# Three small matrix-product jobs inside an attention block are re-cut: compression in two runs, compressed scores with the keys held in the array, high and low values side by side

## The chip, the core and the metric

The kernel runs on one core of a Trainium2 chip. The core has a matrix engine (TensorE: PE in the profile, with PEld for its weight loads), a vector engine (DVE), a scalar engine (ACT), GpSimd (POOL) and a queue engine that issues transfers (SP). The metric is device microseconds of the whole program, one launch. Before the change the median of three runs is 1295.36 us (1295.05 to 1295.36).

A matrix product holds one operand in the 128x128 array (the stationary one, brought in by a weight load) and streams the other past it; the sum goes to one of eight banks of PSUM.

## The reference

Two layers of a transformer trunk on 256 tokens of width 1024, all in fp32. Each layer does, in this order: a gated feed-forward block, an attention block with three branches, a second feed-forward block and a small gated input. The time of this case is decided in the attention block:

```python
ya = diff_attention(aq, ak, av, ...)   # A: 4 heads, two softmaxes each, values 128 wide, then a norm per head
yb = nsa_attention(...)                # B: 8 heads in 2 groups: compressed + selected + window attention
yc = swa_sink_attention(cq, ck, cv)    # C: 8 heads in 2 groups, window 128, sinks
merged = sigmoid(ga)*(ya@w0) + sigmoid(gb)*(yb@w1) + sigmoid(gc)*(yc@w2)
h = h + merged @ w_out
```

The compressed part of B takes blocks of 32 tokens (step 16, so 15 blocks) of its keys and of its values, adds a position, multiplies each by a 2048x256 matrix, applies gelu and multiplies by a 256x64 matrix:

```python
k_cmp = gelu((blocks(kc) + pos[0]) @ cmp_w1[0]) @ cmp_w2[0]      # and the same for the values
p_c = masked_softmax(q . k_cmp * scale + bias, dist_c >= 0)
o_c = p_c @ v_cmp
```

## The kernel before

**Precision.** Most products are made of three: each operand is split into a high and a low part (type fp32r), and `mul3` (lines 264 to 267) adds high x high, high x low and low x high. ACT makes the high part by a copy (line 258), DVE the low part by a subtraction (line 253). A few products, the compression among them, are done on plain fp32 operands instead; the trace shows each of those as two matrix instructions.

**Main line and side lines.** The large products of the attention block (projections A0, A1, A2, Ck, Cq, Bk, Bv, Bq, then for each branch the gate and the branch product, two column halves each, then the output product) are emitted one after the other by `product`. After each step of three matrix instructions it calls `flow.tick()`. `Flow` (line 186) holds side lines, which are Python generators: at each tick a lane gets `pace` more credit, and for every whole credit one step (up to the next `yield`) of its first side line is emitted. Lane 0 holds the attention of A, then C, then B, with paces `PACE_A`, `PACE_C`, `PACE_B` (line 47); lane 1 holds the compressed part with pace 1. `flow.join` emits what is left of a side line when its result is needed.

The order in which things are emitted is their priority. A planner then sets the order on each engine: it goes through a simulated time line and takes, on each engine, the instruction of best priority whose operands and buffers are free. `tc.high_priority(offset=n)` moves an instruction n places ahead in priority, and `keep_in_program_order` keeps it behind the one before it. On the chip each engine then works through its own list in order.

**Weights.** All streamed weights go through one list, `queue`, fetched in its order (`fetch`, line 303), at least `AHEAD` places in front of their use. A streamed piece (512 KB) lands in one of 4 `raw` tiles by a transfer on SP, and its high and low part go to one `wh` and one `wl` tile, 6 of each (`WBUFS`). The eight pieces of the compression matrix (`Whole`, line 382) are not split: they land directly in `wh` tiles (even pieces) and `wl` tiles (odd pieces). They enter the list behind other pieces: `Weights.push` (lines 288 to 292) takes one of them for every second piece of Bv, Bq and what follows.

**Compression** (`compressing`, line 1181). The tile `e` (token blocks with the position added) is stationary in quarters of the array: 32 columns at a time, so that key and value and two successive row blocks go to the four column groups. For each of the eight weight pieces, as soon as it is there, four fp32 products of 256 columns are emitted (line 1202), then the side line yields. All add up in one PSUM bank (`cmp`), one of three with the tag `tp`. Then follow gelu and the second matrix (`compressed`, line 1207), and the compressed keys `kbd` are split into high and low, `kt`.

**Compressed scores** (`attend_cmp`, line 1280), once per half of the tokens (`t` = 0, 1): four `mul3` with the queries stationary (128x128) and 32 columns of keys streaming, then bias, softmax and gate on DVE and ACT at [128, 8, 16], a transpose by the matrix engine (`pct`) and a copy to `pcT[t]`, which the attention of B waits for.

**Values of A** (`attend_a`, `second`, line 1093). For each of four units (head pair m, token half t), and for each of two heads and t + 1 key blocks, one `mul3` with the transposed probabilities stationary and 128 value columns streaming, into the single bank with the tag `y`. Then two squares with row sums straight from that bank (line 1107), mean and power -1/2 (POOL, line 1109), the scaling out of the bank (line 1110), two transposes (`yt`) and a split.

**Scores of A, B and C** (`scores`, line 996) use the array in two row halves of 64 and write twelve products to two banks (tag `s`). The first has its natural priority, the other eleven are 300 places ahead and kept in order.

Of the kernel before, what the change touches and what calls it, by code (L numbers as in the profile page):

```python
# [43 lines left out]
LATE_ON = False  # L44
FLIPS = ["flip"]
POINTS = (5, 8, 11, 14, 18, 21)
PACE_A, PACE_B, PACE_C = 0.8, 0.8, 0.8

# [166 lines left out]
def trunk(ctx: ExitStack, tc: tile.TileContext, a: dict, out: bass.AP, index: list):  # L217
# [24 lines left out]
    def y_bank(name):  # L242
        return bank("y", 1, name)
# [20 lines left out]
    def mul3(ps, xh, xl, wh, wl, start, stop, **kw):  # L264
        nc.tensor.matmul(ps, xh, wh, start=start, stop=False, **kw)  # L265
        nc.tensor.matmul(ps, xh, wl, start=False, stop=False, **kw)  # L266
        nc.tensor.matmul(ps, xl, wh, start=False, stop=stop, **kw)  # L267
# [10 lines left out]
    class Weights:  # L278
# [9 lines left out]
        def push(self, j):  # L288
            self.at[j] = len(queue)
            queue.append(lambda: self.tiles.__setitem__(j, load(*self.pieces[j], 2 if self.at[j] < 2 else 1, j in self.apart)))  # L290
            if extra and j % 2 == 0:
                extra.pop(0)()

        def __call__(self, k):
# [659 lines left out]
    def attention(i, norm, after):  # L954
# [116 lines left out]
        def attend_a():  # L1071
            bnd = band(0)

            def first(u):
                m, t = u
                nk = 128 * (t + 1)
                s = scores("s", qk[m], [0, 1], t, lambda x, r, k: qk[m][r, x, 2 + k, :nk])
                yield
                p = pool.tile([128, 4, 256], F32, tag="p", bufs=3, name="p")
                st = None  # L1080
                for st in softmax([p[:, j, :nk] for j in range(4)], [s[j // 2][:, j % 2, :nk] for j in range(4)],
                                  [back(bnd[:, 2 * m + j % 2], nk) for j in range(4)]):
                    yield
                nc.vector.reciprocal(st[:, 8:12], st[:, 4:8])
                nc.vector.tensor_scalar(st[:, 10:12], st[:, 10:12], nlam[:, i:i + 1], None, op0=ALU.mult)
                for x in range(2):
                    nc.vector.tensor_scalar(p[:, 2 + x, :nk], p[:, 2 + x, :nk], st[:, 10 + x:11 + x], None, op0=ALU.mult)
                    nc.vector.scalar_tensor_tensor(p[:, x, :nk], p[:, x, :nk], st[:, 8 + x:9 + x], p[:, 2 + x, :nk],
                                                   op0=ALU.mult, op1=ALU.add)
                yield  # L1090
                return p

            def second(u, p):
                m, t = u
                T = turned([p[:, x, k * 128:(k + 1) * 128] for k in range(t + 1) for x in range(2)])
                yield
                y_ps = y_bank("ya")[:, :256]
                for x in range(2):
                    o, hd = slice(x * 128, x * 128 + 128), slice((2 * m + x) * 128, (2 * m + x + 1) * 128)
                    for k in range(t + 1):  # L1100
                        mul3(y_ps[:, o], T[:, 0, 2 * k + x, :], T[:, 1, 2 * k + x, :], va[0][:, 0, k, hd], va[0][:, 1, k, hd], k == 0, k == t)
                    yield
                y = pool.tile([128, 256], F32, tag="yt", bufs=2, name="yn")
                st = pool.tile([128, 32], F32, tag="st", bufs=4, name="st")
                for x in range(2):
                    o = slice(x * 128, x * 128 + 128)
                    nc.scalar.activation(y[:, o], y_ps[:, o], AF.Square, accum_out=st[:, x:x + 1])
                nc.vector.tensor_scalar(st[:, 2:4], st[:, 0:2], 1.0 / 128, EPS, op0=ALU.mult, op1=ALU.add)
                nc.gpsimd.tensor_tensor(st[:, 4:6], st[:, 2:4], mhalf[:, :2], op=ALU.pow)
                nc.vector.tensor_tensor(y.rearrange("p (h e) -> p h e", h=2), y_ps.rearrange("p (h e) -> p h e", h=2),  # L1110
                                        st[:, 4:6, None].to_broadcast([128, 2, 128]), op=ALU.mult)
                yield
                if m == 0:
                    yA[t] = y_tile("yA")
                ps = tp_bank("yt")
                transposes(ps, [y[:, x * 128:x * 128 + 128] for x in range(2)])
                split(yA[t][:, 0, 2 * m:2 * m + 2], yA[t][:, 1, 2 * m:2 * m + 2],
                      ps[:, :256].rearrange("p (k q) -> p k q", k=2), sg[:, i:i + 1])
                yield

            yield from pipelined([(m, t) for m in range(2) for t in range(NT)], first, second)


# [57 lines left out]
        def compressing():  # L1181
            pos = pool.tile([128, 2, 2, 8], F32, name="pos")
            nc.sync.dma_start(pos, a["pos"][i].rearrange("p (v s j) -> p v s j", v=2, s=2))
            e = base.tile([128, 2, 2, 8, 32], F32, tag="blk", bufs=6, name="e")
            yield
            nc.vector.memset(e[:, :, 1, :, 31:32], 0.0)
            for kv in range(2):
                for s in range(2):
                    nc.vector.tensor_tensor(
                        e[:, kv, s, :, 0:32 - s],  # L1190
                        half[0][:, 2 * kv:2 * kv + 2, :].rearrange("p g (n j) -> p j (g n)", j=8)[:, :, s:],
                        pos[:, kv, s, :, None].to_broadcast([128, 8, 32 - s]), op=ALU.add)
                yield
            c_ps = bank("tp", 3, "cmp")
            for j in range(8):
                while not w1.ready(j, 3):
                    yield
                w = w1(j)
                for x in range(4):
                    k, kv = 2 * j + x // 2, x % 2  # L1200
                    q = 32 * (2 * (k % 2) + kv)
                    nc.tensor.matmul(c_ps[q:q + 32, :256], e[:, kv, k // 8, k % 8], w[:, 256 * x:256 * x + 256], start=j == 0, stop=j == 7)
                yield
            c_sb[0] = pool.tile([128, 256], F32, name="c_sb")
            nc.vector.tensor_copy(c_sb[0], c_ps[:, :256])

        def compressed():
# [29 lines left out]
            kv_ = k_ps[:, :32].rearrange("p (g n) -> p g n", g=2)  # L1237
            nc.vector.tensor_copy(kbd[0:64, :, 0:16], kv_[0:64])
            nc.vector.tensor_copy(kbd[64:128, :, 16:32], kv_[64:128])
            kt = pool.tile([128, 2, 2, 32], F32R, name="kc")  # L1240
            split(kt[:, 0], kt[:, 1], kbd)
            yield
            v_ps = tp_bank("vc")
            rows_ = base.tile([128, 2, 2, 128], F32R, tag="stage", bufs=4, name="rows")
# [9 lines left out]
            yield  # L1254
            vc[0] = pool.tile([128, 1, 128], F32R, name="vc")
            values(vc[0], v_ps[:, :64], None)
            kc[0] = kt
            yield
            for t in range(NT):
                yield from attend_cmp(t)  # L1260

        def weighted(y_ps, v, T, start, stop):

# [13 lines left out]

        yB, pcT, readyB = [None] * NT, {}, [0] * NT

        def attend_cmp(t):  # L1280
            s_ps = tp_bank("sc")
            for j in range(4):
                mul3(s_ps[:, 32 * j:32 * j + 32], qB[0][:, 0, j, t * 128:(t + 1) * 128], qB[0][:, 1, j, t * 128:(t + 1) * 128],
                     kc[0][:, 0, j // 2], kc[0][:, 1, j // 2], True, True)
            yield
            p = pool.tile([128, 8, 16], F32, tag="pc", bufs=2, name="pc")
            st = pool.tile([128, 32], F32, tag="st", bufs=4, name="st")
            nc.vector.tensor_tensor(p, s_ps[:, :128].rearrange("p (h n) -> p h n", h=8), cbias[:, t], op=ALU.add)
            nc.vector.tensor_reduce(st[:, 0:8], p, axis=AX.X, op=ALU.max)
            nc.vector.tensor_tensor(p, p, st[:, 0:8, None].to_broadcast([128, 8, 16]), op=ALU.subtract)  # L1290
            nc.scalar.activation(p, p, AF.Exp)
            yield
            nc.vector.tensor_reduce(st[:, 8:16], p, axis=AX.X, op=ALU.add)
            nc.vector.reciprocal(st[:, 8:16], st[:, 8:16])
            nc.vector.tensor_tensor(st[:, 0:8].rearrange("p (g a b) -> p g a b", g=2, a=2),
                                    st[:, 8:16].rearrange("p (g a b) -> p g a b", g=2, a=2),
                                    sig[t][:, 0:8].rearrange("p (g b a) -> p g a b", g=2, a=2), op=ALU.mult)
            nc.vector.tensor_tensor(p, p, st[:, 0:8, None].to_broadcast([128, 8, 16]), op=ALU.mult)
            nc.vector.tensor_tensor(p, p, cmask[:, None, t, :].to_broadcast([128, 8, 16]), op=ALU.mult)
            yield  # L1300
            ps = tp_bank("pct")
            transposes(ps, [p.rearrange("p h n -> p (h n)")])
            pcT[t] = pool.tile([128, 128], F32, tag="pcT", bufs=2, name="pcT")
            nc.scalar.activation(pcT[t], ps[:, :128], AF.Copy)
            yield

        def own(t, g):
# [453 lines left out]
```

## Time and profile before

| what | value |
|---|---|
| median of 3 runs | 1295.36 us |
| the profiled execution, its own time | 1295.46 us |
| its span (first to last instruction) | 1293.7 us |
| matrix instructions in it | 6250 |
| TensorE clock granted, mean | 0.998 |
| stretch with the side lines, layer 1, about | 210 to 420 us of the span |
| stretch with the side lines, layer 2, about | 847 to 1057 us of the span |

In the views, an instruction group is named by line, engine, operation, output and inputs. In the timeline the first number is the start and the second the time that the group is in flight. Matrix instructions are pipelined, so a new one starts long before the last one ends; what one costs the engine is the distance from its start to the start of the next.

### The profile page before, as it was taken

How to read it: one execution, taken by the hardware profiler on the slowest of the kernel's cores; microseconds unless marked ns; L12 is line 12 of the kernel's file. 1: busy time of each engine (PE TensorE's matmuls, PEld its weight loads, DVE VectorE, ACT ScalarE, POOL GpSimd, SP SyncE). 2: the span in 40 equal slices, each digit the busy share in tenths (PEclk: the TensorE clock that was granted, in tenths of full speed). 3: DMA queues.
4: the chain of work that ended last, by engine and by line, in shares of the span. 5: the costliest groups of instructions: out<-in, count | busy, mean ns of one | idle time of the engine just before them, and what ended most of it. 6: DMA issues, size and time to landing. Idle time of an engine off the chain costs nothing.

```text
span 1293.7 us, 17861 instructions
## 1 busy us (share of the span) xinstructions
PE 1283.7 (99%) x6250; PEld 1052.7 (81%) x6250; DVE 1069.8 (83%) x1736; ACT 907.8 (70%) x1450; POOL 27.5 (2%) x46
## 2 busy tenths in 40 slices
PE   9999999999999999999999999999999999999997
PEld 7888888877878888888888888888778788888886
DVE  7878977666788799997799999777677978999975
ACT  6778667577587487876667876676765866787664
POOL 0000000000000000000000000000000000000000
PEclk9999999999999999999999999999999999999999
DMA  8778788465534568687666787865654435678772
GB/s 320 230 232 269 206 243 224 165 237 167 189 118 129 175 185 244 212 241 214 212 195 237 201 250 229 250 180 200 224 178 144 140 130 194 206 202 240 237 222 83
DMA packets 137179, 263.73 MB, mean 204 GB/s; under 512 B 71670, under 2 KB 77174, under 8 KB 137088
## 3 DMA queue, kind: packets, MB, share of 16 engines
q1 hardware_dynamic: 134128, 252.56, 63.4%
q0 software_dynamic: 2528, 9.47, 2.2%
q8 instruction: 49, 0.80, 0.3%
q10 hardware_dynamic: 432, 0.56, 0.1%
q14 instruction: 42, 0.34, 0.1%
HBM read 245.74 MB, written 1.08 MB: 191 GB/s over the span
## 4 chain that ended last, share of the span: by engine, by line
PE 99%; issue 0%; DVE 0%; ACT 0%; POOLq 0%; POOL 0%; DVEq 0%; ACTq 0%
PE ff L266 8%; PE ff L265 8%; PE ff L267 8%; PE fo L267 5%; PE fo L265 5%; PE fo L266 5%; PE p L265 4%; PE p L267 4%; PE p L266 4%; PE gate L265 4%; PE gate L266 4%; PE gate L267 4%; PE s L1008 2%; PE br L265 2%; PE A L266 2%; PE A L267 2%
## 5 line engine op out<-in xcount | busy, mean ns | idle before, releaser
L253 DVE TENSOR_TENSOR wl<-raw,wh 128x1024 fp32r<-128x1024 f32 (+1 forms) x410 | 491.8, 1213 | 85.2 <-ACT wh L258 84.2
L258 ACT ACTIVATE wh<-raw 128x1024 fp32r<-128x1024 f32 (+1 forms) x410 | 424.7, 1048 | 155.0 <-DMA raw<-in_wst 59.1
L266 PE MATMUL ff<-wl,nT 128*128 128x512 f32 x464 | 180.9, 390 | 0.0
L267 PE MATMUL ff<-wh,nT 128*128 128x512 f32 x464 | 180.3, 390 | 0.0
L265 PE MATMUL ff<-wh,nT 128*128 128x512 f32 x464 | 171.7, 390 | 0.0
L267 PE MATMUL fo<-wh,gT 128*128 128x512 f32 x304 | 117.1, 390 | 0.0
L266 PE MATMUL fo<-wl,gT 128*128 128x512 f32 x304 | 115.7, 389 | 0.0
L265 PE MATMUL fo<-wh,gT 128*128 128x512 f32 x304 | 114.3, 390 | 0.0
L266 PEld LDWEIGHTS ff<-wl,nT 128*128 128x128 f32 x464 | 87.1, 188 | 18.2 <-DVE wl L253 0.3
L265 PEld LDWEIGHTS ff<-wh,nT 128*128 128x128 f32 x464 | 87.1, 188 | 18.0
L267 PEld LDWEIGHTS ff<-wh,nT 128*128 128x128 f32 x464 | 87.1, 188 | 17.9
L265 PE MATMUL gate<-wh,nT 128*128 128x512 f32 x192 | 78.3, 408 | 0.0
L266 PE MATMUL gate<-wl,nT 128*128 128x512 f32 x192 | 76.8, 400 | 0.0
L267 PE MATMUL gate<-wh,nT 128*128 128x512 f32 x192 | 76.8, 402 | 0.0
L267 PEld LDWEIGHTS fo<-wh,gT 128*128 128x128 f32 x304 | 57.1, 188 | 11.8
L266 PEld LDWEIGHTS fo<-wl,gT 128*128 128x128 f32 x304 | 57.1, 188 | 11.8
L265 PEld LDWEIGHTS fo<-wh,gT 128*128 128x128 f32 x304 | 57.1, 188 | 11.7
L1021 ACT ACTIVATE p<-p,st 128x128 f32<-128x128 f32 (+1 forms) x128 | 56.6, 446 | 13.2 <-DVE st L1019 12.1
L606 ACT ACTIVATE whole<-flip 128x1024 uint16<-128x1024 uint16 x32 | 43.0, 1367 | 20.9 <-DMA flip<-cut 20.9
L600 ACT ACTIVATE cut<-gated 128x1024 uint16<-128x1024 uint16 (+1 forms) x48 | 46.3, 974 | 8.6 <-DVE gated L646 8.6
L253 DVE TENSOR_TENSOR wl<-x,wh 128x1024 fp32r<-128x1024 f32 x42 | 50.5, 1224 | 2.0 <-ACT wh L258 2.0
L258 ACT ACTIVATE wh<-x 128x1024 fp32r<-128x1024 f32 x42 | 43.8, 1049 | 5.7 <-DVE x L253 4.5
(391 smaller groups left out, 2734.0 us busy)
## 6 DMA issues: line engine op xcount, KB each, us to landing
raw<-in_wst SPq DMA_DIRECT2D x408, 512.0 KB, 4.4
w<-in_wst SPq DMA_DIRECT2D x16, 512.0 KB, 4.6
y<-in_wst POOLq DMA_DIRECT2D x6, 1024.0 KB, 6.6
band<-table SPq DMA_DIRECT2D x10, 512.0 KB, 4.7
xy<-in_wst POOLq DMA_DIRECT2D x4, 512.0 KB, 4.1
raw<-in_wbv SPq DMA_DIRECT2D x4, 420.0 KB, 3.1
xt<-in_xt SPq DMA_DIRECT2D x4, 256.0 KB, 5.5
raw<-in_wst SPq DMA_DIRECT2D x4, 256.0 KB, 5.2
```

The costliest lines, as they stand in the source:

```text
L253: nc.vector.tensor_tensor(o, x, y, op=ALU.subtract)
L258: nc.scalar.activation(hi, src, AF.Copy)
L265: nc.tensor.matmul(ps, xh, wh, start=start, stop=False, **kw)
L266: nc.tensor.matmul(ps, xh, wl, start=False, stop=False, **kw)
L267: nc.tensor.matmul(ps, xl, wh, start=False, stop=stop, **kw)
L600: nc.scalar.activation(cut.rearrange("p (w n) -> p w n", w=2), halves(src)[:, :128 * m].rearrange("p n w -> p w n"), AF.Copy)
L606: tc.keep_in_program_order(nc.vector.tensor_copy(to, of) if late else nc.scalar.activation(to, of, AF.Copy))
L1008: ins = nc.tensor.matmul(o, q[r, x, qb[m], t * 128:(t + 1) * 128], kk, start=x + y == 0, stop=x == 1)
L1021: nc.scalar.activation(p[j], p[j], AF.Exp, bias=st[:, j:j + 1], scale=-1.0, accum_out=st[:, n + j:n + j + 1])
```

## The change

Five edits, all but the first two inside the attention block's side lines:

1. The paces become 0.75 (A), 0.9 (B) and 1.178 (C) instead of 0.8 each.
2. `Weights.push` takes a piece of the compression matrix with every piece pushed, instead of every second one. The list is then Bv0 w0 Bv1 w1 Bv2 w2 Bq0 w3 Bq1 w4 Bq2 w5 Bq3 w6 and, behind the first gate piece, w7; before, the last pieces stood among those of the second gate.
3. The compression waits for four pieces and then emits sixteen products at once, twice; all but the first of each sixteen are 600 places ahead in priority and kept in program order.
4. The compressed scores are made once for both token halves: keys `kbd` (fp32, 32 columns) are stationary in the four column groups, and the high and then the low queries of all 256 tokens stream past, read as plain fp32. The scores come out with heads and blocks on partitions; ACT copies them out, the matrix engine transposes them back (two transposes, new), and bias, softmax, gate, mask, transposes and copy run once at [128, 2, 8, 16].
5. The values of A: the high probabilities are stationary for high and low values side by side (256 columns, two results), then the low ones for the high values (128 columns). ACT copies the low result out, DVE adds the high one; squares and scaling then read the sum from SBUF instead of PSUM.

```diff
-PACE_A, PACE_B, PACE_C = 0.8, 0.8, 0.8
+PACE_A, PACE_B, PACE_C = 0.75, 0.9, 1.178
...
-            if extra and j % 2 == 0:
+            if extra and j % 1 == 0:
...
-                        mul3(y_ps[:, o], T[:, 0, 2 * k + x, :], T[:, 1, 2 * k + x, :], va[0][:, 0, k, hd], va[0][:, 1, k, hd], k == 0, k == t)
+                        nc.tensor.matmul(y_ps[:, x], T[:, 0, 2 * k + x, :], va[0][:, :, k, hd], start=k == 0, stop=False, skip_group_check=True)
+                        nc.tensor.matmul(y_ps[:, x, 0], T[:, 1, 2 * k + x, :], va[0][:, 0, k, hd], start=False, stop=k == t, skip_group_check=True)
...
+                nc.scalar.activation(yv, y_ps[:, :, 1], AF.Copy)
+                nc.vector.tensor_tensor(yv, yv, y_ps[:, :, 0], op=ALU.add)
...
-            for j in range(8):
-                while not w1.ready(j, 3):
+            for b in range(0, 8, 4):
+                while not w1.ready(b + 4 - 1, 3):
                     yield
...
+                        with tc.high_priority(offset=600 if (k, kv) != (2 * b, 0) else 0):
+                            ins = nc.tensor.matmul(c_ps[q:q + 32, :256], e[:, kv, k // 8, k % 8], w[k // 2 - b][:, o:o + 256], start=k < 2, stop=k >= 14)
+                        if (k, kv) != (2 * b, 0):
+                            tc.keep_in_program_order(ins)
...
-        def attend_cmp(t):
+        def attend_cmp():
             s_ps = tp_bank("sc")
-            for j in range(4):
-                mul3(s_ps[:, 32 * j:32 * j + 32], qB[0][:, 0, j, t * 128:(t + 1) * 128], qB[0][:, 1, j, t * 128:(t + 1) * 128],
-                     kc[0][:, 0, j // 2], kc[0][:, 1, j // 2], True, True)
+            for x in range(2):
+                for j in range(4):
+                    with tc.high_priority(offset=0 if x == j == 0 else 300):
+                        ins = nc.tensor.matmul(s_ps[32 * j:32 * j + 32, :SEQ], kc[0][:, j // 2], qB[0][:, x, j].bitcast(F32), start=x == 0, stop=x == 1)
+                    if (x, j) != (0, 0):
+                        tc.keep_in_program_order(ins)
...
+            nc.scalar.activation(sc, s_ps[:, :SEQ], AF.Copy)
+            yield
+            ps = tp_bank("st")
+            transposes(ps, [sc[:, t * 128:(t + 1) * 128] for t in range(NT)])
```

More of the change, by code (lines that the diff above doesn't have):

```diff
@@ L1096, in second @@
                 yield
-                y_ps = y_bank("ya")[:, :256]
+                y_ps = y_bank("ya").rearrange("p (h x e) -> p h x e", h=2, x=2)
                 for x in range(2):
-                    o, hd = slice(x * 128, x * 128 + 128), slice((2 * m + x) * 128, (2 * m + x + 1) * 128)
+                    hd = slice((2 * m + x) * 128, (2 * m + x + 1) * 128)
                     for k in range(t + 1):
-                        mul3(y_ps[:, o], T[:, 0, 2 * k + x, :], T[:, 1, 2 * k + x, :], va[0][:, 0, k, hd], va[0][:, 1, k, hd], k == 0, k == t)
+                        nc.tensor.matmul(y_ps[:, x], T[:, 0, 2 * k + x, :], va[0][:, :, k, hd], start=k == 0, stop=False, skip_group_check=True)
+                        nc.tensor.matmul(y_ps[:, x, 0], T[:, 1, 2 * k + x, :], va[0][:, 0, k, hd], start=False, stop=k == t, skip_group_check=True)
                     yield
@@ L1104, in second @@
                 st = pool.tile([128, 32], F32, tag="st", bufs=4, name="st")
+                yv = y.rearrange("p (h e) -> p h e", h=2)
+                nc.scalar.activation(yv, y_ps[:, :, 1], AF.Copy)
+                nc.vector.tensor_tensor(yv, yv, y_ps[:, :, 0], op=ALU.add)
+                sq = pool.tile([128, 256], F32, tag="ysq", bufs=1, name="sq")
                 for x in range(2):
                     o = slice(x * 128, x * 128 + 128)
-                    nc.scalar.activation(y[:, o], y_ps[:, o], AF.Square, accum_out=st[:, x:x + 1])
+                    nc.scalar.activation(sq[:, o], y[:, o], AF.Square, accum_out=st[:, x:x + 1])
                 nc.vector.tensor_scalar(st[:, 2:4], st[:, 0:2], 1.0 / 128, EPS, op0=ALU.mult, op1=ALU.add)
                 nc.gpsimd.tensor_tensor(st[:, 4:6], st[:, 2:4], mhalf[:, :2], op=ALU.pow)
-                nc.vector.tensor_tensor(y.rearrange("p (h e) -> p h e", h=2), y_ps.rearrange("p (h e) -> p h e", h=2),
-                                        st[:, 4:6, None].to_broadcast([128, 2, 128]), op=ALU.mult)
+                nc.vector.tensor_tensor(yv, yv, st[:, 4:6, None].to_broadcast([128, 2, 128]), op=ALU.mult)
                 yield
@@ L1194, in compressing @@
             c_ps = bank("tp", 3, "cmp")
-            for j in range(8):
-                while not w1.ready(j, 3):
+            for b in range(0, 8, 4):
+                while not w1.ready(b + 4 - 1, 3):
                     yield
[L1198 to L1202, printed above, removed]
+                w = [w1(j) for j in range(b, b + 4)]
+                for k in range(2 * b, 2 * b + 2 * 4):
+                    for kv in range(2):
+                        q, o = 32 * (2 * (k % 2) + kv), 256 * (2 * (k % 2) + kv)
+                        with tc.high_priority(offset=600 if (k, kv) != (2 * b, 0) else 0):
+                            ins = nc.tensor.matmul(c_ps[q:q + 32, :256], e[:, kv, k // 8, k % 8], w[k // 2 - b][:, o:o + 256], start=k < 2, stop=k >= 14)
+                        if (k, kv) != (2 * b, 0):
+                            tc.keep_in_program_order(ins)
                 yield
@@ L1239, in compressed @@
             nc.vector.tensor_copy(kbd[64:128, :, 16:32], kv_[64:128])
-            kt = pool.tile([128, 2, 2, 32], F32R, name="kc")
-            split(kt[:, 0], kt[:, 1], kbd)
             yield
@@ L1256, in compressed @@
             values(vc[0], v_ps[:, :64], None)
-            kc[0] = kt
+            kc[0] = kbd
             yield
-            for t in range(NT):
-                yield from attend_cmp(t)
+            yield from attend_cmp()
         def weighted(y_ps, v, T, start, stop):
@@ L1278, in attention @@
         yB, pcT, readyB = [None] * NT, {}, [0] * NT
-        def attend_cmp(t):
+        def attend_cmp():
             s_ps = tp_bank("sc")
-            for j in range(4):
-                mul3(s_ps[:, 32 * j:32 * j + 32], qB[0][:, 0, j, t * 128:(t + 1) * 128], qB[0][:, 1, j, t * 128:(t + 1) * 128],
-                     kc[0][:, 0, j // 2], kc[0][:, 1, j // 2], True, True)
-            yield
-            p = pool.tile([128, 8, 16], F32, tag="pc", bufs=2, name="pc")
-            st = pool.tile([128, 32], F32, tag="st", bufs=4, name="st")
[L1288 to L1291, printed above, removed]
-            yield
[L1293 to L1299, printed above, removed]
@@ new lines, in attend_cmp @@
+            for x in range(2):
[4 more added lines that the diff above has]
+                        tc.keep_in_program_order(ins)
+            yield
+            sc = pool.tile([128, SEQ], F32, tag="sc", bufs=1, name="sc")
+            nc.scalar.activation(sc, s_ps[:, :SEQ], AF.Copy)
@@ new lines, in attend_cmp @@
+            yield
+            ps = tp_bank("st")
+            transposes(ps, [sc[:, t * 128:(t + 1) * 128] for t in range(NT)])
+            yield
+            p = pool.tile([128, NT, 8, 16], F32, tag="pc", bufs=1, name="pc")
+            st = pool.tile([128, 32], F32, tag="st", bufs=4, name="st")
+            flat = p.rearrange("p t h n -> p (t h) n")
+            nc.vector.tensor_tensor(flat, ps[:, :SEQ].rearrange("p (h n) -> p h n", n=16), cbias.rearrange("p t h n -> p (t h) n"), op=ALU.add)
@@ new lines, in attend_cmp @@
+            nc.vector.tensor_reduce(st[:, 0:16], flat, axis=AX.X, op=ALU.max)
+            nc.vector.tensor_tensor(flat, flat, st[:, 0:16, None].to_broadcast([128, 16, 16]), op=ALU.subtract)
+            nc.scalar.activation(flat, flat, AF.Exp)
+            yield
+            nc.vector.tensor_reduce(st[:, 16:32], flat, axis=AX.X, op=ALU.add)
+            nc.vector.reciprocal(st[:, 16:32], st[:, 16:32])
+            for t in range(NT):
+                nc.vector.tensor_tensor(st[:, 8 * t:8 * t + 8].rearrange("p (g a b) -> p g a b", g=2, a=2),
+                                        st[:, 16 + 8 * t:24 + 8 * t].rearrange("p (g a b) -> p g a b", g=2, a=2),
+                                        sig[t][:, 0:8].rearrange("p (g b a) -> p g a b", g=2, a=2), op=ALU.mult)
@@ L1300, in attend_cmp @@
+            yield
+            nc.vector.tensor_tensor(flat, flat, st[:, 0:16, None].to_broadcast([128, 16, 16]), op=ALU.mult)
+            nc.vector.tensor_tensor(p, p, cmask[:, :, None, :].to_broadcast([128, NT, 8, 16]), op=ALU.mult)
             yield
             ps = tp_bank("pct")
-            transposes(ps, [p.rearrange("p h n -> p (h n)")])
-            pcT[t] = pool.tile([128, 128], F32, tag="pcT", bufs=2, name="pcT")
-            nc.scalar.activation(pcT[t], ps[:, :128], AF.Copy)
+            transposes(ps, [p[:, t].rearrange("p h n -> p (h n)") for t in range(NT)])
@@ L1305, in attend_cmp @@
+            both = pool.tile([128, NT, 128], F32, tag="pcT", bufs=1, name="pcT")
+            nc.scalar.activation(both.rearrange("p t q -> p (t q)"), ps[:, :SEQ], AF.Copy)
+            for t in range(NT):
+                pcT[t] = both[:, t]
             yield
```

## The prediction

> **What bounds the kernel now.** I read the page first, then who waited for whom, then the stretches, and at the end the timeline of TensorE around the lines that the change touches.
>
> ```profile
> span 1293.7 us, 17861 instructions
> PE 1283.7 (99%) x6250; PEld 1052.7 (81%) x6250; DVE 1069.8 (83%) x1736; ACT 907.8 (70%) x1450; POOL 27.5 (2%) x46
> PE 99%; issue 0%; DVE 0%; ACT 0%; POOLq 0%; POOL 0%; DVEq 0%; ACTq 0%
> ```
>
> TensorE is in use through 1283.7 of 1293.7 us, and the chain that ended last is 99% its own: nearly every matrix instruction was released by the one before it. Matrix instructions overlap, so "busy" alone could hide waits. The list of waits, for PE alone, and two stretches rule that out:
>
> ```profile
> PE warm L1703 <- DVE idle L1698: 1.5, 1, 1.5
> ...
> 210.00:420.00 210.00, 210.00 (x1198) 169.57 (x1197) 160.11 (x401) 148.16 (x344) 2.77 (x4) 1.00 0.53 170
> ...
> 847.00:1057.00 210.00, 210.00 (x1198) 169.67 (x1197) 160.35 (x401) 148.13 (x344) 2.77 (x4) 1.00 0.53 170
> ```
>
> The only wait is at the start of the program. The stretches that hold the side lines (columns: length, PE, PEld, DVE, ACT, POOL, clock, DMA share, GB/s) have the same counts in both layers, so what one costs is counted twice. DVE is free for 50 of 210 us there, ACT for 62, the transfers for half. So the time is the sum of the distances from one matrix start to the next, and I cost the change in these distances.
>
> **Compression in two runs.** The timeline of PE:
>
> ```profile
> 282.82 1.91 PE L1202 MATMUL cmp<-w,e 128*32 128x256 f32 x26
> 284.67 0.32 PE L1008 MATMUL s<-kC,qC 64*128 64x128 f32 x1
> 284.92 0.64 PE L1202 MATMUL cmp<-w,e 128*32 128x256 f32 x8
> 285.49 0.88 PE L1008 MATMUL s<-kC,qC 64*128 64x128 f32 x11
> 286.30 0.63 PE L1202 MATMUL cmp<-w,e 128*32 128x256 f32 x6
> 286.86 0.50 PE L265 MATMUL gate<-wh,nT 128*128 128x512 f32 x1
> ...
> 288.42 0.62 PE L1202 MATMUL cmp<-w,e 128*32 128x256 f32 x2
> ...
> 289.39 0.63 PE L1202 MATMUL cmp<-w,e 128*32 128x256 f32 x6
> ...
> 299.51 0.64 PE L1202 MATMUL cmp<-w,e 128*32 128x256 f32 x8
> ...
> 308.06 0.63 PE L1202 MATMUL cmp<-w,e 128*32 128x256 f32 x6
> ...
> 312.38 0.40 PE L267 MATMUL gate<-wh,nT 128*128 128x512 f32 x1
> 312.71 0.62 PE L1202 MATMUL cmp<-w,e 128*32 128x256 f32 x2
> 313.26 0.50 PE L265 MATMUL gate<-wh,nT 128*128 128x512 f32 x1
> 313.59 0.40 PE L266 MATMUL gate<-wl,nT 128*128 128x512 f32 x1
> 313.82 0.39 PE L267 MATMUL gate<-wh,nT 128*128 128x512 f32 x1
> ```
>
> The 64 records of a layer (32 products, two each) fall into eight runs. A run of 2, 6 or 8 records lasts 0.55, 0.56 or 0.57 us to the next start (312.71 to 313.26, 286.30 to 286.86, 284.92 to 285.49): up to four products go through the four column groups side by side, and one costs as much as four. A run of 26 lasts 1.85: three full groups of 8 and a run of 2, so a full group inside a run costs (1.85 - 0.55) / 3 = 0.43. Each run also lengthens its neighbours: the gate before takes 0.33 (312.38 to 312.71) and the one after 0.33 (313.26 to 313.59) where a gate takes 0.23 (313.59 to 313.82). That is 0.10 at each edge.
>
> Before, per layer: the block from 282.82 to 286.86 is 4.04, with outer edges 4.24; in it is one set of scores of C, whose last eleven take 0.81 and which, whole and with edges, I put at 1.02. This leaves 3.22. The other five runs (2, 6, 8, 6, 2) are 2.79 and with edges 3.79. Together 7.01. After: a run of 32 is 3 x 0.43 + 0.57 = 1.86, with edges 2.06, two of them 4.12. Saved 2.89 a layer, **5.8 us** in both. Less, if runs break (a rival below).
>
> **Compressed scores.** Before, 24 instructions a layer, in two blocks of twelve:
>
> ```profile
> 350.06 0.26 PE L265 MATMUL sc<-kc,qB 128*128 128x32 f32 x1
> ...
> 351.40 0.48 PE L265 MATMUL gate<-wh,nT 128*128 128x512 f32 x1
> ```
>
> Twelve take 1.34, so 0.112 each and 2.69 a layer. After, eight fp32 products of the compression's shape (32 columns stationary, 256 streaming): one run of two groups, 0.43 + 0.57 = 1.00, with edges 1.20; and two more transposes. Four transposes are 0.36 (248.19 to 248.55, quoted next), two 0.18. Saved 2.69 - 1.38 = 1.31 a layer, **2.6 us**. I take the compression's row because the shape is the same; the bounds are two groups side by side as there, or all eight one by one at a lone product's 0.55 (4.4 + 0.2, a loss of 2.1 a layer). The row of the same shape decides.
>
> In the Trainium skill ("TensorE: Matmul & The Clock Gate", section "Measured speedup vs the span model") three column tiles give 2.38 times, 0.79 of the ideal. By that a group would cost 0.43 / 0.79 = 0.54, and the 20 groups of the new runs in both layers 20 x 0.11 = 2.2 us more than I count (an estimate). The trace has four products for the price of one, and goes before it.
>
> **High and low values side by side.**
>
> ```profile
> 248.19 0.60 PE L273 MATMUL qt<-ident,stage 128*128 128x128 f32 x4
> 248.55 0.31 PE L265 MATMUL ya<-va,pT 128*128 128x128 f32 x1
> ...
> 249.92 0.45 PE L267 MATMUL Bk<-wh,nT 128*128 128x512 f32 x1
> ```
>
> ```profile
> 222.90 0.28 PE L265 MATMUL Ck<-wh,nT 128*128 128x256 f32 x1
> 223.02 0.28 PE L266 MATMUL Ck<-wl,nT 128*128 128x256 f32 x1
> ```
>
> A `mul3` of 128 columns is 3 x 0.114 = 0.34 (twelve instructions from 248.55 to 249.92). A product of 256 columns costs 0.12 (the Ck row), so the pair costs 0.12 + 0.11 = 0.23. There are 12 a layer (2 pairs x 2 heads x 1 + 2 key blocks): saved 1.3 a layer, **2.6 us**; other ya blocks run a little closer than 0.114, so I take 2.4. That the 256 columns come from two places is not in the trace: the bounds are 0.11 (as for 128) and 0.23 (as for 512), which moves 2.4 between 2.6 and -0.2.
>
> It adds, per unit and eight times in all, a copy on ACT and an add on DVE, at 128x256 out of PSUM:
>
> ```profile
> L1110 DVE TENSOR_TENSOR yn<-ya,st x8: 416/425/458, 237.0 to 916.9; 128x256 f32<-128x256 f32 x8
> ```
>
> About 0.43 each, 3.4 us on each engine, between the last ya instruction and the yt transposes. The main products hide them on PE and the 50 and 62 free us on DVE and ACT; without that cover it is 0.85 a unit, 6.8 us. The softmax of the compressed part becomes one chain of wider operations where two stood, and the split of the keys falls away: fewer instructions on DVE, off the path, nothing. The bank of the values comes free earlier, before POOL's power instead of after it.
>
> **Paces and the list of weights.** These two cost nothing by themselves; they move work. The price at stake is a set of scores broken in two:
>
> ```profile
> 279.60 0.38 PE L1008 MATMUL s<-kC,qC 64*128 64x256 f32 x1
> 279.91 0.49 PE L265 MATMUL gate<-wh,nT 128*128 128x512 f32 x1
> 280.34 0.98 PE L1008 MATMUL s<-kC,qC 64*128 64x256 f32 x11
> 281.24 0.50 PE L266 MATMUL gate<-wl,nT 128*128 128x512 f32 x1
> ...
> 392.75 0.38 PE L1008 MATMUL s<-kB,qB 64*128 64x256 f32 x1
> ```
>
> The first product goes alone (0.31), a gate gets in (0.43 instead of 0.23), eleven follow: 0.51 more than a whole set. Between these two rows six of a layer's fourteen sets are broken so (two of C, four of B), beside the one at 284.67 that the compression broke. None of A is. The breaks come where the second bank is free later than the first. Faster paces could bring sets closer to the softmax that frees the banks, or C's work ahead of the crowd with the compression. Bounds: none broken, -12 x 0.51 = -6.1; all broken, +16 x 0.51 = +8.2. From the rows I see no reason for one sign and take 0.
>
> Three transfers of the compression matrix move ahead, past the pieces of Bq and the first gates in SP's list.
>
> ```profile
> raw<-in_wst SPq DMA_DIRECT2D x408, 512.0 KB, 4.4
> ```
>
> The transfers are at 0.53 of their time there, so the move is free on them; what it does to the tiles is the rival on the slow side.
>
> **The sum.** -5.8 - 2.6 - 2.4 = -10.8. The profiled execution took 1295.46 by its own time (1.8 more than its span), 0.1 above the median 1295.36. Forecast: 1295.4 - 10.8 = **1284.6 us**, its own range 1282 to 1287.
>
> **The rivals.**
>
> *Fewer broken sets.* C is done sooner at 1.178 and the compression no longer cuts in, so half or more of the twelve broken sets could become whole; for it speaks that four of A's four are whole, where the banks are not pressed; against it the higher pace of B, which has most breaks. All: 1284.6 - 6.1 = 1278.5.
>
> *The runs break.* As in `scores`, the first product of each new run has its natural priority, and only the rest is pulled ahead. If each of the six runs loses its first product, each costs a lone 0.55 and edges 0.2 more: 6 x 0.75 = 4.5, 1289.1. So the change would not quite do what its words say. For it: half of the score sets break. Against: these write one bank, the sets two, and the weights must be in before the first is emitted.
>
> *The saved time comes back as waiting.* PE gains 10.8 us, and the stretch then hangs on DVE or ACT: 1295.4. Against: 50 free us.
>
> *The tiles run out: slower.* A piece of the compression matrix sits in a `wh` or `wl` tile from its landing to its run. Before, it went as soon as it was in; now four wait for each other, two of the six tiles of each kind, up to three with the next. Bq needs four pieces at once for its two token halves. If the first run is late (it waits for `e`), a piece of Bq or of the first gate finds no tile, SP's list stands behind it, and PE waits for a landing and a split:
>
> ```profile
> L253 DVE TENSOR_TENSOR wl<-raw,wh 128x1024 fp32r<-128x1024 f32 (+1 forms) x410 | 491.8, 1213 | 85.2 <-ACT wh L258 84.2
> L258 ACT ACTIVATE wh<-raw 128x1024 fp32r<-128x1024 f32 (+1 forms) x410 | 424.7, 1048 | 155.0 <-DMA raw<-in_wst 59.1
> ```
>
> 4.4 + 1.05 + 1.21 = 6.7, less the 12 x 0.23 = 2.8 that PE still has from the piece before: 3.9 for each starved piece. With two a layer it is 1284.6 + 15.6 = 1300.2; from three in all it ends slower than before (3 x 3.9 = 11.7 against 10.8). Against: `raw` tiles take landings ahead, and PE can do the second half's products of pieces that are in.
>
> **How the numbers follow.** My forecast 0.56; fewer broken sets 0.17; runs break 0.13; waiting 0.07; tiles 0.07. A measurement here tells about 0.2%, 2.6 us, from no change. Faster holds the first three, 0.86; same 0.07; slower 0.07. The range leaves the last two out (0.14) and ends near the two others and their unknown prices: 1278 to 1290.5.
>
> **What would show it.** Right: 6214 matrix instructions (24 fewer ya, 16 fewer sc, 4 more transposes); the cmp line in four runs of 32, each 1.86 to the next start; sc in two runs of 16 at 1.0; ya pairs 0.12 and 0.11 apart; still no wait on PE. Wrong, if a run of x2 stands alone ahead of one of x30, if PE waits for `wl` or for a transfer between 262 and 300, or if the count of lone s rows moves far from six a layer.

## The result, and the profile after

The changed kernel takes 1285.41 us (median of four runs, 1285.08 to 1285.68) against 1295.36 before (four runs by now, 1295.05 to 1296.23): 9.95 us less, a ratio of 0.9922 with a 95% interval of 0.9905 to 0.9939. The forecast was 1284.6. The page of the changed kernel, whose profiled execution took 1285.68:

```profile
span 1283.9 us, 17792 instructions
PE 1271.9 (99%) x6214; PEld 1044.5 (81%) x6214; DVE 1069.8 (83%) x1728; ACT 908.7 (71%) x1454; POOL 28.9 (2%) x46
...
PE 92%; DMA 2%; ACT 2%; DVE 2%; issue 1%; SPq 0%; POOLq 0%; POOL 0%; DVEq 0%; ACTq 0%
```

There are 6214 matrix instructions, as counted. What is new is the chain that ended last: 8% of it is no longer PE. That is not 8% of lost time. Wherever PE waits, the chain goes back through the engine that it waited for, and most of its pieces off PE lie between 88 and 146 us, far from the change, behind one wait of 0.4 (`fo`, at 146.05). What was lost is in the list of waits of PE (waiting line, what released it, us in total, times, longest):

```profile
PE warm L1721 <- DVE idle L1716: 1.5, 1, 1.5
PE ya L1102 <- DVE pT L253: 0.7, 1, 0.7
PE gate L266 <- DVE wl L253: 0.6, 2, 0.3
PE fo L265 <- ACT wh L258: 0.4, 1, 0.4
PE ff L712 <- ACT nT L469: 0.3, 1, 0.3
PE Bq L265 <- ACT sig L1162: 0.2, 1, 0.2
```

They come to 3.7 us, 1.5 of them at the start of the program. Before, the first of these was the only one. To see where the time went, take in each layer the stretch from the first instruction of the product Ck to the last of the output product. Timeline of PE, before:

```profile
221.01 0.39 PE L265 MATMUL Ck<-wh,nT 128*128 128x256 f32 x1
...
445.22 0.39 PE L267 MATMUL wo<-wh,mT 128*128 128x512 f32 x1
...
1082.15 0.39 PE L267 MATMUL wo<-wh,mT 128*128 128x512 f32 x1
```

and after:

```profile
221.51 0.39 PE L265 MATMUL Ck<-wh,nT 128*128 128x256 f32 x1
...
441.34 0.39 PE L267 MATMUL wo<-wh,mT 128*128 128x512 f32 x1
...
1072.78 0.39 PE L267 MATMUL wo<-wh,mT 128*128 128x512 f32 x1
```

Layer 1 goes from 224.2 to 219.8, layer 2 (its Ck starts at 858.08 before and 854.21 after) from 224.1 to 218.6: 4.4 and 5.5 less, where the working gave 5.4 each. The rest of the program is as it was to half a microsecond.

The three parts in the timeline of the changed kernel. The compression, in layer 1:

```profile
298.61 0.38 PE L1008 MATMUL s<-kC,qC 64*128 64x256 f32 x1
298.93 0.33 PE L273 MATMUL pt<-ident,p 128*128 128x128 f32 x1
299.18 1.93 PE L1207 MATMUL cmp<-w,e 128*32 128x256 f32 x32
301.05 0.97 PE L1008 MATMUL s<-kC,qC 64*128 64x256 f32 x11
...
302.43 1.93 PE L1207 MATMUL cmp<-w,e 128*32 128x256 f32 x32
304.29 0.66 PE L273 MATMUL pt<-ident,p 128*128 128x128 f32 x4
```

Two whole runs of 32 records, 1.87 and 1.86 to the next start, as worked out. The first stands in the middle of a broken set of C's scores. The compressed scores:

```profile
342.55 1.07 PE L1289 MATMUL sc<-qB,kbd 128*32 128x256 f32 x16
343.55 0.50 PE L266 MATMUL br<-wl,yC 128*128 128x512 f32 x1
```

One run of 16 records, 1.00. The values of A, in a unit that runs through and in the one that does not (both layer 1):

```profile
250.45 0.22 PE L1102 MATMUL ya<-va,pT 128*128 128x128 f32 x1
250.51 0.33 PE L1101 MATMUL ya<-va,pT 128*128 128x256 f32 x1
250.68 0.22 PE L1102 MATMUL ya<-va,pT 128*128 128x128 f32 x1
250.74 0.33 PE L1101 MATMUL ya<-va,pT 128*128 128x256 f32 x1
...
263.39 0.28 PE L1101 MATMUL ya<-va,pT 128*128 128x256 f32 x1
264.38 0.33 PE L1102 MATMUL ya<-va,pT 128*128 128x128 f32 x1 [0.71 <-DVE pT L253]
```

A pair costs 0.17 + 0.06 = 0.23 (250.51 to 250.74), the sum that was forecast. At 263.39 the next instruction starts 0.99 later, because the low probabilities are not there. DVE made the low half of a weight piece and a part of B's values first, and these low probabilities only then:

```profile
262.50 1.23 DVE L253 TENSOR_TENSOR wl<-raw,wh 128x1024 fp32r<-128x1024 f32 x1 [1.03 <-ACT wh L258]
...
263.91 0.41 DVE L253 TENSOR_TENSOR pT<-pt,pT 128x256 fp32r<-128x256 f32 x1
```

Layer 2 has no such wait. A second one, at a gate, is in both layers (287.80 here):

```profile
286.88 0.61 PE L265 MATMUL gate<-wh,nT 128*128 128x512 f32 x2
287.80 0.50 PE L266 MATMUL gate<-wl,nT 128*128 128x512 f32 x1 [0.31 <-DVE wl L253]
```

Two starts and the gap after them take 0.92 where two gates take 0.46. What DVE and ACT did before it:

```profile
283.51 1.06 ACT L258 ACTIVATE wh<-raw 128x1024 fp32r<-128x1024 f32 x1 [1.80 <-PE gate L267]
...
284.28 0.67 DVE L1193 TENSOR_TENSOR e<-half,pos 128x256 f32<-128x256 f32 x1 [1.31 <-issue]
...
284.85 1.76 DVE L1193 TENSOR_TENSOR e<-half,pos 128x248 f32<-128x248 f32 x3
286.53 1.22 DVE L253 TENSOR_TENSOR wl<-raw,wh 128x1024 fp32r<-128x1024 f32 x1
```

The high half of the piece came late, after ACT had waited 1.80 for a product of the gate, and its low half then stood on DVE behind the making of the compression's `e`.

### The profile page after: what moved, and what is told of

The parts are those of the page before. It is cut to its first block, busy times and chain, and to the rows that moved or that the text cites. A ratio compares the mean times of both kernels' runs of the same rounds, so it can differ in the third digit from the quotient of the medians.

```text
span 1283.9 us, 17792 instructions
## 1 busy us (share of the span) xinstructions
PE 1271.9 (99%) x6214; PEld 1044.5 (81%) x6214; DVE 1069.8 (83%) x1728; ACT 908.7 (71%) x1454; POOL 28.9 (2%) x46
## 4 chain that ended last, share of the span: by engine, by line
PE 92%; DMA 2%; ACT 2%; DVE 2%; issue 1%; SPq 0%; POOLq 0%; POOL 0%; DVEq 0%; ACTq 0%
PE ff L267 7%; PE ff L266 7%; PE ff L265 7%; PE fo L265 5%; PE fo L266 5%; PE fo L267 5%; PE p L265 4%; PE p L266 4%; PE p L267 4%; PE gate L267 3%; PE gate L266 3%; PE gate L265 3%; PE s L1008 2%; PE br L266 2%; PE br L265 2%; PE A L266 2%
## 5 line engine op out<-in xcount | busy, mean ns | idle before, releaser
L267 PE MATMUL gate<-wh,nT 128*128 128x512 f32 x192 | 76.0, 398 | 0.0
L265 PE MATMUL gate<-wh,nT 128*128 128x512 f32 x192 | 75.2, 399 | 0.0
```

## The experiments

Four kernels carry a part of the change on the kernel before (edits 2 and 3 go together), four are the changed kernel with one edit, or in one case half of edit 3, taken back, and four move the first product of a set of scores. The changed kernel without edit 4 alone was not run. Each ran beside the kernel before on the same chip; ratios are to that. "Stretch" is the two stretches of above taken together: 448.3 us before, 438.4 after. A layer has fourteen sets of scores; broken sets count as two runs, and all runs of a layer are counted, 21 before and 20 after.

**High and low side by side, alone** (edit 5 on the kernel before)

```diff
-mul3(y_ps[:, o], T[..0..], T[..1..], va[0][:, 0, k, hd], va[0][:, 1, k, hd], ...)
+nc.tensor.matmul(y_ps[:, x], T[:, 0, 2 * k + x, :], va[0][:, :, k, hd], ...)
+nc.tensor.matmul(y_ps[:, x, 0], T[:, 1, 2 * k + x, :], va[0][:, 0, k, hd], ...)
```

> The kernel before with edit 5 alone (high and low values of A side by side). Theory of start distances: a mul3 of 3 x 0.11 becomes a pair of 0.23, twelve a layer, 2.4 to 2.6 us less in all: 1292.9. Rival, the longer chain on ACT and DVE is not hidden: eight units of 0.85 us in part on the path, 1294 to 1299, with waits of PE for yt or pT. Rival, edit 5 is what made PE wait for the split of pT in layer 1 of the changed kernel (the 0.99 us start distance at 263 us): then that wait is here too.

1296.58, ratio 1.0009 (1.0000 to 1.0019): no gain. PE waits for neither yt nor pT, so both rivals fall, and the ya instructions are 1.0 and 1.1 us shorter in the two layers (start distances summed). But sets of scores are broken that were whole. The fourteen sets of a layer are 23 and 24 runs here, 21 before. One of A, in the timeline:

```profile
242.22 0.38 PE L1008 MATMUL s<-qkA 64*128 64x256 f32 x1
242.96 0.97 PE L1008 MATMUL s<-qkA 64*128 64x256 f32 x11
```

Five more breaks at 0.51 are 2.6 us, and the compression's runs, cut in other places, are 0.4 longer a layer. That is 3.4 lost against 2.1 gained, and the medians are 1.3 apart. The gain is there and is spent in the order.

**Compressed scores, alone** (edit 4 on the kernel before)

```diff
-mul3(s_ps[:, 32 * j:32 * j + 32], qB[..t..], ..., kc[0][:, 0, j // 2], kc[0][:, 1, j // 2], True, True)
+nc.tensor.matmul(s_ps[32 * j:32 * j + 32, :SEQ], kc[0][:, j // 2], qB[0][:, x, j].bitcast(F32), start=x == 0, stop=x == 1)
```

> The kernel before with edit 4 alone (compressed scores with the keys stationary, both halves at once). Theory of start distances: 24 x 0.112 become one run of 16 records at 1.0 with edges 0.2 and two transposes at 0.18, 1.3 a layer: 1292.8. Rival, column groups shared worse than in the compression: a run of 16 longer than 1.0, less gain. Rival, the one chain delays the part that the attention of B waits for: less gain, and PE waits in the stretch of B.

1293.0, ratio 0.9982 (0.9973 to 0.9991): 2.3 less, nearly the forecast, by three things. The products gain what was said, four breaks fewer (19 runs of scores a layer) gain 2.0, and a new wait takes away 1.2 in each layer:

```profile
PE mt L273 <- DVE merged L1463: 1.5, 2, 0.7
```

It stands at the hand-over to the output product: the starts at 416.38 and 416.81 take 1.63 together where two take 0.46. B's last value product is at 413.86 by then, where in the kernel before the last ones stood at 419.26 and later, and filled the time in which DVE and ACT make the merged values ready. That this is why PE waits fits the rows, but no run tested it.

**List and two runs, alone** (edits 2 and 3 on the kernel before)

```diff
-if extra and j % 2 == 0:
+if extra and j % 1 == 0:
...
-for j in range(8):
+for b in range(0, 8, 4):      # sixteen products, pulled ahead and in order
```

> The kernel before with edits 2 and 3 alone (list of weights and two runs of sixteen). Theory of start distances: eight runs of compression become two, 2.9 us a layer: 1289.6. Rival, the matrix tiles kept longer starve the stream of weights: PE waits for wl or for a transfer between 262 and 300 us, 3.9 us each.

1287.74, ratio 0.9943 (0.9928 to 0.9958): 7.6 less (the interval is 5.4 to 9.3), more than the 5.8. Two runs of 32 in each layer, and the sets of scores are 18 runs a layer instead of 21. Six breaks fewer are 3.1, of which the 5.8 already held two. No wait for `wl` or a transfer in the stretch: the tiles do not run out.

**Paces, alone** (edit 1 on the kernel before)

```diff
-PACE_A, PACE_B, PACE_C = 0.8, 0.8, 0.8
+PACE_A, PACE_B, PACE_C = 0.75, 0.9, 1.178
```

> The kernel before with edit 1 alone (paces 0.75, 0.9, 1.178). Theory of start distances: no instruction is added or taken away, 0 within 1 us: 1295.4, and the number of lone first score products decides the sign at 0.5 each. Rival, the paces are where the gain comes from (work of C ahead of the crowd): 1290 or less. Rival, they cost: C is pressed and PE waits for DVE around 263 us: 1296 to 1298.

1292.99, ratio 0.9983 (0.9973 to 0.9992): 2.3 less with the same 6250 instructions. The compression falls into six runs a layer instead of eight, and scores into 20 instead of 21. The runs of the compression are 0.28 shorter in all and have four edges of 0.10 less, a break is 0.51: together 1.2 a layer, which is what the stretches lost (445.9 in all). The zero of the prediction was wrong for the kernel before.

**The changed kernel without side by side**

```diff
 (the changed kernel, with mul3 for the values of A and squares from PSUM as before)
```

> The changed kernel without edit 5 (three products per pair as before). Theory of start distances: 2.4 us more than the changed kernel: 1287.8, unless the wait for pT in layer 1 is edit 5's, in which case it goes too and it is 1286.7.

1295.04, ratio 1.0000 (0.9991 to 1.0009): all of the gain is gone, 9.6 us instead of the 2.4 expected. The stretch is 6.6 longer than in the changed kernel (445.0). Of that, the ya instructions are 0.9 (7.65 against 6.75, which holds the 0.99 wait). The start distances of the output product are 3.3 longer, mostly by waits at the hand-over that the changed kernel does not have:

```profile
PE wo L266 <- DVE wb L253: 2.2, 2, 1.7
...
PE wo L265 <- ACT wb L258: 0.4, 1, 0.4
```

In layer 2 another 0.8 is eight transposes of the next block that stand inside the stretch here.

The profiled execution is the fastest of its runs (1293.49), so 1.5 of the 9.6 is not in this trace. Why the order comes out so without edit 5 was not settled.

**The changed kernel with all paces at 0.8**

```diff
-PACE_A, PACE_B, PACE_C = 0.75, 0.9, 1.178
+PACE_A, PACE_B, PACE_C = 0.8, 0.8, 0.8
```

> The changed kernel with all paces at 0.8. Theory of start distances: within 1 us of the changed kernel, 1284.4 to 1286.4; if the paces made the waits of PE (about 1.2 us at 263 us in layer 1, 0.5 us at 287 us and at 919 us), these go and it is 1283 to 1284. Rival, the other edits only pay with the paces: 1288 or more.

1284.08, ratio 0.9913 (0.9899 to 0.9928): the best of all, though its interval overlaps the changed kernel's. Waits for pT and at the gate are gone (DVE makes `e` from 279.92 on here, not from 284.28), scores are 18 and 19 runs against 20 and 20. So the paces, a gain on the kernel before, are none once the other edits are in.

**The changed kernel with the old list**

```diff
-if extra and j % 1 == 0:
+if extra and j % 2 == 0:
```

> The changed kernel with one piece of the compression matrix for every second piece pushed, as before. The runs come later (the second behind the second gate's pieces). Theory of start distances: the same number of matrix instructions in the same runs, 0 within 1 us: 1285.4. Rival, the early list holds tiles that the stream needs, and the waits at 263, 287 and 919 us are its price: 1283 to 1284 here. Rival, the late second run comes after the scores of B should start and these wait: 1287 or more.

1291.58, ratio 0.9972 (0.9962 to 0.9982): 6.2 more, of which the stretches show 4.3 (442.7). The runs are whole but start at 307.40 and 310.28 in layer 1 instead of 299.18 and 302.43, and PE waits in many places:

```profile
PE mt L273 <- DVE merged L1470: 0.7, 1, 0.7
PE yt L273 <- DVE st L1433: 0.7, 1, 0.7
PE wo L266 <- DVE wb L253: 0.6, 1, 0.6
```

The second stands behind DVE's work for the softmax of C (at 295.8), the others at the hand-over; 0.7 at a feed-forward product lies outside the stretches. They are not waits for weights alone. The early list is not what made PE wait; without it there is more of it.

**The changed kernel with the runs not pulled ahead**

```diff
-with tc.high_priority(offset=600 if (k, kv) != (2 * b, 0) else 0):
+with tc.high_priority(offset=0):
...
-if (k, kv) != (2 * b, 0):
-    tc.keep_in_program_order(ins)
```

> The changed kernel with the sixteen products of a run at their natural priority and free in their order, as the products of the compression were before. Theory: what makes the run whole is that all sixteen are emitted at once, so only a few break off; each further run costs 0.75 us, 0 to 3 us in all: 1285.4 to 1288.4. Rival, the pulling makes it: runs fall apart as before the change, 1290.

1290.6, ratio 0.9964 (0.9951 to 0.9977): 5.2 more. The compression of layer 1:

```profile
298.16 1.48 PE L1207 MATMUL cmp<-w,e 128*32 128x256 f32 x18
...
300.95 1.49 PE L1207 MATMUL cmp<-w,e 128*32 128x256 f32 x20
...
302.63 0.63 PE L1207 MATMUL cmp<-w,e 128*32 128x256 f32 x4
...
303.45 0.64 PE L1207 MATMUL cmp<-w,e 128*32 128x256 f32 x8
...
304.28 0.63 PE L1207 MATMUL cmp<-w,e 128*32 128x256 f32 x4
...
305.09 1.05 PE L1207 MATMUL cmp<-w,e 128*32 128x256 f32 x10
```

Six runs instead of two, in both layers: eight more at 0.64. The rival was right. Emitting sixteen at once does not keep them together. The pulling and the kept order, taken away together here, do; which of the two was not tested. The waits of the changed kernel (pT 0.7, gate 0.6) are here too, so the pulling is not their cause.

**Scores kept whole.** If breaks cost 0.51, a kernel without them must gain. The first product of a set is put back in priority, so that it goes only when the other eleven can follow; once on the kernel with paces 0.8, once on the changed kernel, once on the kernel before.

```diff
-with tc.high_priority(offset=0 if (m, x, y, par) == (0, 0, 0, 0) else 300):
+with tc.high_priority(offset=-150 if (m, x, y, par) == (0, 0, 0, 0) else 300):   # -300 on the changed kernel
```

> The changed kernel with all paces at 0.8 and the first score product of each set 150 places back in priority, so that it goes only when the other eleven can follow. All 28 sets of the two layers should be whole. Theory of start distances: the nine breaks of the kernel with all paces at 0.8 go at 0.51 us each, 4.6 us: 1284.1 - 4.6 = 1279.5. Rival, a break costs nothing because PE would wait elsewhere: 1284. Rival, scores that go later delay their softmax, and the end of a branch or of the attention waits: 1285 or more.

> The changed kernel, paces as changed, with the first score product of each set 300 places back. Theory of start distances: of twelve breaks some four stay, 8 x 0.51 = 4.1 us less: 1281.3. Rival as above: 1285.4 or more.

> The kernel before with the first score product of each set 150 places back. Theory of start distances: 14 breaks become about 2, 12 x 0.51 = 6.1 us less, if the compression keeps its eight runs a layer: 1289.3. Rival, what the sets gain the compression loses, since it is cut in more runs at 0.75 us: 1292 to 1297.

1285.1 (0.9917, 0.9900 to 0.9933), 1292.11 (0.9970, 0.9960 to 0.9981) and 1297.46 (1.0010, 1.0001 to 1.0019). None gains on the kernel that it was made from (1284.08, 1285.41 and 1295.65). In the first all 28 sets are whole, and the score instructions are 1.1 us a layer shorter; but PE now waits, mostly near the end of the attention. In the second two sets of each layer, both of C, are still broken. The waits of the first, and those of the second, without the 1.5 at the start:

```profile
PE wo L265 <- ACT wb L258: 2.0, 2, 1.0
...
PE yb L1268 <- ACT pT L258: 0.9, 2, 0.5
PE Bv L265 <- ACT stage L1138: 0.7, 1, 0.7
```

```profile
PE mt L273 <- DVE mT L262: 1.5, 2, 0.8
PE br L265 <- DVE th L1469: 1.5, 2, 0.8
...
PE pt L273 <- DVE p L1368: 1.4, 2, 0.7
PE yb L1269 <- DVE pT L253: 1.0, 2, 0.5
```

In the third the compression of layer 2 is cut into ten runs, beside the same kind of waits. The last set of B in layer 1 starts at 400.9, 402.6 and 404.4 in the three, against 387.2, 390.4 and 392.7 in the kernels that they were made from. A set that goes later starts its softmax later, and what follows it on DVE and ACT comes too late for PE. The rival that said so fits: a broken set is a cost, and also the price for an early start.

**The late bank first**

```diff
-for par in range(2):
+for par in (1, 0):      # and the first product, at natural priority, is now that of par 1
```

> The changed kernel with the order of the two banks in a set of scores turned round: the product for the bank that the softmax frees last goes first. The prediction put the breaks down to the second bank coming free later than the first; then no set is broken now, 12 x 0.51 = 6.1 us less: 1279.3. Rival, the breaks come from the lower priority of the first product alone: the same twelve breaks, 1285.4.

1285.03 in one run, with 20 runs of scores a layer, cut in the same places as in the changed kernel. The order of the banks does not make the breaks; the prediction's reason for them falls. That the low priority of the first product takes part is shown by the kernels above, in which putting it further back made sets whole; why only some break at natural priority is left open.

## Why the prediction was right, and where it was wrong

**What bounds the kernel: right.** In the changed kernel as in the one before, the time is the sum of start distances on PE, and work added off PE did not show: PE waits nowhere for the transposes `yt`, which come after the added copy and add.

**The prices: right.** A run of 32 is 1.86 (forecast 1.86), the run of compressed scores 1.00 (1.00), a pair 0.23 (0.23), the instructions 6214 (6214), lone first products six a layer (six). Of the pair only the sum holds: the signs named parts of 0.12 and 0.11, and they are 0.17 and 0.06. Four column groups of compressed scores cost what the compression's row said. The Trainium skill ("TensorE: Matmul & The Clock Gate", section "Measured speedup vs the span model") gives three column tiles 2.38 times, 0.79 of the ideal. The prediction's estimate from it would have made the run of 16 about 1.2, and it took 1.00. This does not test the page's figure itself: the 0.43 that the estimate divided by 0.79 was measured with four products side by side already.

**The sum: 10.8 forecast, 9.95 measured.** Layer 2 gave 5.5 of its 5.4. Layer 1 gave 4.4: about 1.2 went into the waits at 263 to 265 (0.99 and 0.41 where 0.17 and 0.06 are usual) and each layer lost 0.5 at the gate. So the sign "still no wait on PE" did not hold. The prediction had such waits only as its rival "the saved time comes back", at full price; 2.1 came back, a fifth. With these waits taken off, each layer gained 6.0, which is 0.6 more than the sum holds, in small differences that were not followed up. The two misses partly cancel, which is luck.

**Broken runs: the rival did not come, for the reason that was only half given.** The first product of a run did not go alone. The one bank that was named as the reason was not tested; what was shown is that without the pulling and the kept order the runs fall apart at 0.64 apiece, near the 0.75 given.

**Tiles run out: its sign came, at a small part of its price.** The prediction named a wait of PE for `wl` between 262 and 300 as a sign of being wrong. There is one, at 287.80: 0.31 instead of the 3.9 of a starved piece. ACT had waited for a product of the gate ahead of that piece, which may be a tile that came free late, and the making of `e` stood in front of its low half. The kernel with paces 0.8 has the same early list and no such wait, and taking the early list back made the kernel slower by 6.2. So the list did not starve PE.

**Paces at 0: the step that failed in the reasoning.** "From the rows I see no reason for one sign and take 0" turned out a gain of 2.3 on the kernel before, and no gain (1.3 the other way, not told apart) on top of the other edits. The bounds, -6.1 and +8.2, were about the right size, but they belong to every edit, not to this one: each edit makes the planner set a new order, and the order is worth as much as the edit. The single edits alone come to +1.3, -2.3, -7.6 and -2.3, together -10.9 and near the whole, but taking one back costs 9.6, 6.2 and 5.2 or gains 1.3. That the forecast of the whole came within 1 us is therefore in part luck: with the score breaks, cuts of the compression or hand-over waits of a neighbouring kernel it would have been up to 10 us off.

## What to carry to other kernels

Where one engine is never idle, cost an edit in the distances between its starts: runs of the same shape gave prices here that held to a hundredth of a microsecond. Where a planner sets the order anew for each edit, give the whole a range for the order as well, and look after the fact at three things that it changes: how often small sets are broken, in how many runs a mode of the array is entered, and whether work is left to fill the hand-over from one stage to the next. An edit that looks worthless alone may be needed in company, so test it in both places.

## What the runs showed of the hardware that was not expected

A product of 256 columns followed by one of 128 with another stationary operand takes 0.17 and then 0.06, not 0.12 and 0.11: the sum holds, the parts do not. A lone score product in the row-half mode with 256 columns costs 0.31 to the next start (298.61 to 298.93), whether a gate, a transpose or, in the kernel with the paces alone, a run of the compression follows; one with 128 columns costs 0.25 (284.67 to 284.92 in the kernel before).
